# A two-layer transformer on one core: two weight splits and five modulation folds issued at other places

## The chip, the cores and the metric

The kernel runs on 1 core of a Trainium2 chip. The metric is the device time of one execution in microseconds. The engines are named as in the profile: PE is TensorE's matmul queue (PEld its weight loads), DVE VectorE, ACT ScalarE, POOL GpSimd, SP the queue that issues the DMAs. Each engine works through its own instructions in order and waits on semaphores for the others.

## The reference

Two layers over 512 latent tokens (`x`) and 256 context tokens (`ctx`), width 1024. Layer 0 mixes with attention, layer 1 with a gated recurrence (HGRN); each is followed by a SwiGLU feed-forward with a hidden width of 2816. Around both stand six modulation vectors, computed from the conditioning.

```python
for i in range(DEPTH):
    last = i == DEPTH - 1
    mod_l = (jax.nn.silu(c) @ ada_w[i] + ada_b[i])[:, None, :]
    mod_c = (jax.nn.silu(c_ctx) @ ada_w[i] + ada_b[i])[None, None, :]
    sh1_l, sc1_l, gt1_l, sh2_l, sc2_l, gt2_l = jnp.split(mod_l, 6, axis=-1)
    ...
    h = h + gt1_l * y_l
    h = h + gt2_l * swiglu(modulate(rms_norm(h, norm_ffn_w[i]), sh2_l, sc2_l), ffn_w_in[i], ffn_w_out[i])
    if not last:
        hc = hc + gt1_c * y_c
        hc = hc + gt2_c * swiglu(modulate(rms_norm(hc, norm_ffn_w[i]), sh2_c, sc2_c),
                                 ffn_w_in[i], ffn_w_out[i])
return rms_norm(h, final_norm_w)

def swiglu(h, w_in, w_out):
    a, u = jnp.split(h @ w_in, 2, axis=-1)
    return (jax.nn.silu(a) * u) @ w_out
```

## The kernel before, in words

**Products.** Every product is made of three matmuls (`mm3`, lines 118 to 120): each operand is split into a high part (a cast to fp32r on ACT, line 90) and a low part (the difference of the original and the high part, on DVE, line 95). `split` does this. With `late="h"` or `"l"` in its argument it pins the cast or the difference: a pinned instruction keeps its place in program order on its engine, while the scheduler may place the others by its own reckoning.

**The first feed-forward** (`ffn` for layer 0) treats the 768 tokens as two halves of 384 columns (`H`), and the 1024 inputs as two halves of four blocks (`b11`, `b12`, `b21`, `b22`: input half, token half). Hidden rows come in tiles `j` of 128. For `j` 0 and 1 the products are plain (`ffi`). From `j` = 2 on a hidden tile is a "pair" of gate and up weights, and is computed with seven block products in place of eight, by sums and differences: x, z, y, x again, w, y again, x again (`m1`, `m2`, `m5`, `m6`, `m4`, `m3`, `m7`). The operands of these are the four input blocks and four differences of them over the tokens, `t1` to `t4`; the differences are formed in place in `start_attention`, `b11 - b12` and `b22 - b12` on POOL (lines 1367 and 1371), then `-b11 - b22` and `-b22 - b21` on DVE (lines 1374 and 1378).

**Units.** The weights of a pair pass in seven units of 512 columns. A unit's `split_next()` makes its two parts in a ring of three tiles, then runs the unit's `after`: behind the first unit (`a11`) POOL makes three weight sums (lines 1220, 1220, 1223; the second of them is the weight of unit three, `raw_('w', 2, 1)`), behind the second (`a12`) a fourth (line 1228). All of these write over the tiles that the units read, so they come after the first two units' low parts. In `start_attention` the first two units are split after all token differences; `split_ahead(0)` splits some more behind the plain products. While `begun[0]` holds (in these start functions), the units' low parts are pinned and the casts are not.

**Around it.** When pair 2 begins, ACT and DVE also finish the hidden rows of tiles 0 and 1 (`plain_hidden`: SiLU at line 1057, the product `c` at line 1058, then `gh` and `gl`, the high and low part of the hidden rows), and split `t2`, `t4` and, before that, `t1`, `t3` (the tiles `xt1h`, `xt1l` and so on).

**Fill.** Between the units runs the fill: `ada_ffn` computes five chunks (0, 1, 2, 3 and 5) of layer 1's modulation on DVE, one step after another at given units. A chunk's steps end with a reduction to `adpart` (line 250). It is then "folded": four small matmuls sum its rows (`folded`, line 257; the profile counts two passes, so 8), and DVE adds the bias into `modc` (line 258). The fold of a chunk is issued some steps into the next chunk, and the last one after some empty steps or at the `drain()` at the end of the feed-forward.

The output products of a part of the hidden rows (`ffo`) follow the part's pairs; a row of them is 512 latent and 256 context columns, and DVE adds it to the residual `hT` (line 760).

## Time and profile before

| | |
|---|---|
| median of the runs | 1803.81 us (1802.84 to 1805.98, 3 runs) |
| profiled execution, span | 1806.6 us |
| PE busy | 1748.6 us, 97% |
| DVE, ACT, POOL busy | 1302.5, 871.2, 640.4 us |
| first feed-forward's pairs begin (first `x` product's end) | 475.1 us |
| third fold (line 257) | 773.7 us |
| the feed-forward's end (first `h` product of the next stage) | 965.5 us |

The profile is one execution, whose span lies 2.8 us above the median of the runs. In a row of the timeline the first number is the start in us from the span's start, the second the duration, then the engine, the line, what is written and read, the shape and how many such instructions the row groups; in brackets stands how long the engine was idle before and what ended it. PEclk is the granted clock of TensorE, 1.00 at full speed.

### The profile page before, as it was taken

The numbers are of one execution on the slowest core, as the hardware profiler recorded it, in microseconds if no ns is written. First come the engines' busy times: TensorE is split into PE (matmuls) and PEld (weight loads), VectorE is DVE, ScalarE is ACT, GpSimd is POOL, SyncE is SP. The second block draws the span as 40 slices with busy tenths as digits, with TensorE's granted clock in tenths as the row PEclk, the third lists the DMA queues.
The fourth block names the chain that finished last, engine by engine and source line by source line (L and its number), as shares of the span: only waits on it lengthen the run. The fifth ranks groups of instructions, "written<-read, shape, count | busy, mean of one in ns | idle before, by whom it ended". The sixth has DMA issues, their size and how long they took to land.

```text
span 1806.6 us, 30621 instructions
## 1 busy us (share of the span) xinstructions
PE 1748.6 (97%) x11717; PEld 1605.0 (89%) x11717; DVE 1302.5 (72%) x2269; ACT 871.2 (48%) x1777; POOL 640.4 (35%) x582
## 2 busy tenths in 40 slices
PE   8989999999999999999999999999999899999998
PEld 6788788898899989999998999899898899999996
DVE  4776688888888878887866555655747658786764
ACT  3454777777533424243346443333434445554444
POOL 1354355435512314121313333234425454333420
PEclk9999999999999999999999999999999899999999
DMA  8543410002034242545331122122211123333322
GB/s 297 202 129 116 153 36 25 24 1 77 24 111 122 71 129 88 159 129 158 96 114 46 59 71 68 51 83 83 80 49 47 57 59 114 100 111 103 100 61 83
DMA packets 213459, 166.43 MB, mean 92 GB/s; under 512 B 7953, under 2 KB 190401, under 8 KB 213313
## 3 DMA queue, kind: packets, MB, share of 16 engines
q1 hardware_dynamic: 213024, 163.43, 29.5%
q8 instruction: 92, 1.51, 0.3%
q10 hardware_dynamic: 288, 1.05, 0.1%
q14 instruction: 55, 0.44, 0.1%
HBM read 162.36 MB, written 2.10 MB: 91 GB/s over the span
## 4 chain that ended last, share of the span: by engine, by line
PE 78%; DVE 9%; ACT 4%; POOL 3%; issue 3%; DMA 2%; SPq 0%; POOLq 0%; DVEq 0%; ACTq 0%
PE ffo L120 5%; PE ffo L118 5%; PE ffo L119 5%; PE x L118 4%; PE x L120 4%; PE x L119 4%; PE pt L787 3%; PE y L120 2%; PE y L118 2%; PE y L119 2%; PE lv L1716 2%; PE hz L118 2%; PE hz L119 2%; PE hz L120 2%; PE sc L729 1%
## 5 line engine op out<-in xcount | busy, mean ns | idle before, releaser
L1723 POOL TENSOR_TENSOR KD<-KD,tot 128x384 f32<-128x384 f32 x96 | 102.7, 1092 | 81.8 <-ACT kc L1706 78.1
L777 POOL TENSOR_SCALAR pf<-pf,st 128x768 f32<-128x768 f32 (+1 forms) x96 | 73.3, 766 | 126.0 <-DVE st L776 89.5
L760 DVE SCALAR_TENSOR_TENSOR hT<-ffo,modc,hT 128x512 f32<-128x512 f32 (+1 forms) x122 | 78.6, 649 | 45.6 <-PE ffo L120 45.5
L120 PE MATMUL ffo<-gh,wlo_w 128*128 128x512 f32 (+1 forms) x304 | 103.2, 340 | 0.0
L119 PE MATMUL ffo<-gl,whi_w 128*128 128x512 f32 (+1 forms) x304 | 102.7, 338 | 0.0
L118 PE MATMUL ffo<-gh,whi_w 128*128 128x512 f32 (+1 forms) x304 | 102.4, 340 | 0.0
L242 DVE SCALAR_TENSOR_TENSOR adacc<-adw,csil,adacc 128x512 f32<-128x512 f32 x98 | 84.5, 871 | 7.9 <-DMA adw<-in_ada_w_dram 7.8
L95 DVE TENSOR_TENSOR ptl<-pt,pth 128x384 fp32r<-128x384 f32 (+1 forms) x160 | 79.9, 524 | 12.8 <-ACT pth L90 11.6
L90 ACT CAST pth<-pt 128x384 fp32r<-128x384 f32 (+1 forms) x160 | 69.7, 460 | 34.2 <-PE pt L787 22.5
L775 ACT ACTIVATE pf<-sc,st 128x768 f32<-128x768 f32 (+1 forms) x96 | 73.3, 764 | 19.0 <-DVE st L773 18.0
L1723 DVE TENSOR_TENSOR QD<-QD,tot 128x256 f32<-128x256 f32 x96 | 51.9, 581 | 41.2 <-PE lv L1716 41.2
L773 DVE TENSOR_REDUCE st<-sc 128x1 f32<-128x768 f32 (+1 forms) x96 | 74.2, 773 | 10.1 <-PE sc L730 8.7
L1706 ACT COPY kc<-KD 128x256 f32<-128x256 f32 x112 | 43.3, 413 | 75.9 <-PE lv L1716 45.8
L787 PE MATMUL pt<-ident,pf 128*128 128x128 f32 x448 | 72.1, 275 | 5.2 <-DVE ptl L95 4.1
L118 PE MATMUL ffo<-gh,foh 128*128 128x512 f32 (+1 forms) x186 | 71.4, 384 | 0.0
L120 PE MATMUL ffo<-gh,fol 128*128 128x512 f32 (+1 forms) x186 | 70.8, 381 | 0.2 <-DVE fol L95 0.2
L119 PE MATMUL ffo<-gl,foh 128*128 128x512 f32 (+1 forms) x186 | 70.9, 381 | 0.0
L1782 POOL TENSOR_SCALAR oss<-oss 128x4 f32<-128x4 f32 (+1 forms) x9 | 4.7, 522 | 181.8 <-DVE oss L1781 181.7
L1716 PE MATMUL lv<-QD,kc 128*128 128x128 f32 x448 | 63.4, 286 | 4.5 <-DVE QD L1723 2.4
L1716 PEld LDWEIGHTS lv<-QD,kc 128*128 128x128 f32 x448 | 58.6, 191 | 8.8 <-issue 4.6
L119 PEld LDWEIGHTS ffo<-gl,whi_w 128*128 128x128 f32 x304 | 57.8, 190 | 6.9
L787 PEld LDWEIGHTS pt<-ident,pf 128*128 128x128 f32 x448 | 51.2, 140 | 13.9 <-issue 6.4
(1114 smaller groups left out, 6794.1 us busy)
## 6 DMA issues: line engine op xcount, KB each, us to landing
adw<-in_ada_w_dram SPq DMA_DIRECT2D x40, 512.0 KB, 4.6
adw<-in_ada_w_dram SPq DMA_DIRECT2D x80, 256.0 KB, 2.8
raw_hz<-in_hgrn_w_in_dram SPq DMA_DIRECT2D x14, 512.0 KB, 3.7
adr<-in_ada_w_dram SPq DMA_DIRECT2D x16, 256.0 KB, 5.2
adr<-in_ada_w_dram SPq DMA_DIRECT2D x8, 512.0 KB, 7.7
raw_wq<-in_attn_w_qkv_dram SPq DMA_DIRECT2D x8, 512.0 KB, 6.8
raw_wo<-in_attn_w_o_dram SPq DMA_DIRECT2D x8, 512.0 KB, 3.5
raw_hv<-in_hgrn_w_in_dram SPq DMA_DIRECT2D x8, 512.0 KB, 4.9
```

What stands on the lines that cost most here:

```text
L95: m = (eng or DVE).tensor_tensor(lo, src, hi.bitcast(F32), op=ALU.subtract)
L118: PE.matmul(ps, ahi, bhi, start=first, stop=False, **kw)
L119: PE.matmul(ps, ahi, blo, start=False, stop=False, **kw)
L120: PE.matmul(ps, alo, bhi, start=False, stop=last, **kw)
L242: pin(DVE.scalar_tensor_tensor(a, raw, cc, a, op0=ALU.mult, op1=ALU.add))
L760: DVE.scalar_tensor_tensor(hT[o][:, a:e], ps, mcol(layer, ch, o, v), hT[o][:, a:e], op0=ALU.mult, op1=ALU.add)
L773: DVE.tensor_reduce(st3[:, 0:1], ps[:, :nk], op=ALU.max, axis=AX.X, negate=True)
L775: ACT.activation(pf, ps[:, :nk], AF.Exp, bias=st3[:, 0:1], accum_out=st3[:, 1:2])
L777: POOL.tensor_scalar(pf, pf, st3[:, 2:3], 1.0, op0=ALU.mult, op1=ALU.mult)
L787: PE.transpose(pt[:, i * P : (i + 1) * P], pf[:, (i0 + i) * P : (i0 + i + 1) * P], ident)
L1716: PE.matmul(ps[:, cs], kc[:, cs], mv, start=True, stop=True)
L1723: eng.tensor_tensor(view, view, f, op=ALU.mult)
```

## The change

Nothing is added and nothing taken out; three things stand elsewhere.

1. In `start_attention` two `split_next()` calls (units `a11` and `a12` of pair 2) stand ahead of the DVE differences `b22` and `b21`, where they stood behind them.
2. In layer 0, from the third unit on, the units split in the start function have their casts pinned as well as their low parts.
3. In `ada_ffn` a fold is issued 12 steps into the next chunk, where it was 5, and the last one waits for up to 12 empty steps.

```diff
@@ def split_next (line 1297)
-            split(g[0], g[1], u["src"](), late="l" if begun[0] else "")
+            split(g[0], g[1], u["src"](), late=("l" if layer or nsplit[0] < 2 else "hl") if begun[0] else "")
@@ def start_attention (from line 1369)
             for i in range(4):
                 b11, b12, b21, b22 = blocks(i)
                 pin(POOL.tensor_tensor(b12, b22, b12, op=ALU.subtract))
+            split_next()
+            split_next()
             for i in range(4):
                 b11, b12, b21, b22 = blocks(i)
                 pin(DVE.scalar_tensor_tensor(b22, b11, -1.0, b22, op0=ALU.mult, op1=ALU.subtract))
...
             for i in range(4):
                 b11, b12, b21, b22 = blocks(i)
                 pin(DVE.scalar_tensor_tensor(b21, b22, -1.0, b21, op0=ALU.mult, op1=ALU.subtract))
-            split_next()
-            split_next()
             xops["t3"] = operand("t3")
@@ def ada_ffn (from line 1523)
                 n += 1
-                if n == 5 and folded:
+                if n == 12 and folded:
                     folded()
                     folded = None
                 yield got
-        for _ in range(5):
+        for _ in range(12):
             yield
         folded()
```

What this moves in the engines' orders is shown at three places. The first is DVE ahead of pair 2: `x_5542` to `x_5581` are the four `b22` blocks, `c` the first half of hidden tile 0, and the row of `wlo_w` the low parts of the first two units.

```order
+L95 TENSOR_TENSOR wlo_w<-raw_('w', 2, 0)_5632,whi_w 128x512 x2
+L1376 SCALAR_TENSOR_TENSOR x_5542<-x_5461,x_5542 128x384
+L1376 SCALAR_TENSOR_TENSOR x_5553<-x_5478,x_5553 128x384
+L1376 SCALAR_TENSOR_TENSOR x_5570<-x_5495,x_5570 128x384
+L1376 SCALAR_TENSOR_TENSOR x_5581<-x_5531,x_5581 128x384
+L1058 TENSOR_TENSOR c_5796<-ffi,c_5796 128x384
 L95 TENSOR_TENSOR xt3l<-x_5461,xt3h 128x384
 L95 TENSOR_TENSOR xt3l<-x_5478,xt3h 128x384
```

Before, the order began with the four differences (then line 1374) and `c`, and the low parts stood here:

```order
-L1378 SCALAR_TENSOR_TENSOR x_5542<-x_5542 128x384
-L1378 SCALAR_TENSOR_TENSOR x_5553<-x_5553 128x384
-L1378 SCALAR_TENSOR_TENSOR x_5570<-x_5570 128x384
-L1378 SCALAR_TENSOR_TENSOR x_5581<-x_5581 128x384
-L95 TENSOR_TENSOR wlo_w<-raw_('w', 2, 0)_5632,whi_w 128x512 x2
```

The two low parts move 12 rows up, to right behind the last `xt1l`; all that stood between moves two instructions down. The order on POOL is the same, but its sums wait for these low parts.

The second place is ACT at the same time: `gh_5815` are the high parts of hidden tile 1, whose two halves come from `c_5842` and `c_5886`; `sw` and `raw_('w', 2, 1)` are weights that POOL has summed.

```order
 L1057 ACTIVATE c_5842<-ffi 128x384
 L1057 ACTIVATE c_5886<-ffi 128x384
-L90 CAST whi_w<-raw_('w', 2, 1)_5634 128x512
-L90 CAST whi_w<-sw_5798 128x512
 L90 CAST gh_5815<-c_5842 128x384
 L90 CAST whi_w<-raw_('w', 2, 1)_5634 128x512
+L90 CAST whi_w<-sw_5785 128x512
+L90 CAST whi_w<-raw_('w', 2, 1)_5634 128x512
 L90 CAST whi_w<-raw_('w', 2, 0)_5632 128x512
+L90 CAST gh_5815<-c_5886 128x384
 L1082 COPY c_5916<-x 128x384
-L90 CAST gh_5815<-c_5886 128x384
```

The cast of `gh` from `c_5842` now comes ahead of the casts of units three and four, behind which it stood, and the second `gh` ahead of the copy of the first product of pair 2.

The third place is PE at the third fold. Before, it stood between the 512 and the 256 columns of one row of output products:

```order
L120 MATMUL ffo<-gh_8254,wlo_w 128x512
L118 MATMUL ffo<-gh_8398,whi_w 128x512
L119 MATMUL ffo<-gl_8399,whi_w 128x512
L120 MATMUL ffo<-gh_8398,wlo_w 128x512
L257 MATMUL adc_8742<-adpart_8446,fold 32x8 x4
L118 MATMUL ffo<-gh_7970,whi_w 128x256
L119 MATMUL ffo<-gl_7971,whi_w 128x256
```

Now it stands within the pairs of the next part:

```order
L120 MATMUL y<-xb22h,wlo_w 128x384
L118 MATMUL y<-xb22h,whi_w 128x384
L119 MATMUL y<-xb22l,whi_w 128x384
L120 MATMUL y<-xb22h,wlo_w 128x384
L257 MATMUL adc_9180<-adpart_8446,fold 32x8 x4
L118 MATMUL x<-xt3h,whi_w 128x384
L119 MATMUL x<-xt3l,whi_w 128x384
```

The other four folds move by the same seven steps; the fifth now stands at the end of the feed-forward, right ahead of the first `h` product. The sixth (chunk 4, in the recurrence) stands where it stood.

## The prediction

> **What bounds the kernel now.** I read the page first, then TensorE's waits between 440 and 970 us, where every edit lies, then the timeline around the two longest of them. The page's busy shares and the engines of its chain of waits:

> ```profile
> PE 1748.6 (97%) x11717; PEld 1605.0 (89%) x11717; DVE 1302.5 (72%) x2269; ACT 871.2 (48%) x1777; POOL 640.4 (35%) x582
> ...
> PE 78%; DVE 9%; ACT 4%; POOL 3%; issue 3%; DMA 2%; SPq 0%; POOLq 0%; DVEq 0%; ACTq 0%
> ```

> TensorE is busy 1748.6 of 1806.6 us, so a reordering can only win from the 58 us in which it stands, and from matmuls that run at a lowered clock. Its waits in that stretch (the kind, us in total, times, longest):

> ```profile
> PE y L120 <- DVE wlo_w L95: 2.3, 1, 2.3
> PE adc L257 <- DVE adpart L250: 2.2, 1, 2.2
> ...
> PE h L118 <- DVE hT L760: 0.8, 1, 0.8
> PE y L118 <- ACT whi_w L90: 0.5, 1, 0.5
> PE w L119 <- DVE xt4l L95: 0.2, 1, 0.2
> ```

> Two places matter: **stall A**, the first product of pair 2 (y, at 478 us), and **stall B**, the third modulation fold (adc, at 774 us). Each is followed by matmuls at half clock, as stretches of 3.41 us show (after each engine its busy us; then PEclk):

> ```profile
> 476.46:479.88 3.42, 1.50 (x8) 0.86 (x6) 0.40 (x1) 2.08 (x5) 3.18 (x3) 1.00 0.00 0
> 479.88:483.29 3.41, 2.50 (x8) 2.50 (x9) 3.14 (x6) 1.22 (x4) 0.00 (x0) 0.50 0.03 9
> 483.29:486.70 3.41, 3.41 (x11) 2.88 (x10) 3.11 (x7) 3.14 (x8) 0.00 (x0) 0.50 0.49 145
> ...
> 770.07:773.48 3.41, 1.45 (x7) 0.83 (x5) 3.41 (x6) 0.00 (x0) 0.00 (x0) 1.00 0.59 173
> 773.48:776.90 3.42, 3.17 (x21) 3.17 (x22) 2.99 (x7) 0.18 (x1) 0.00 (x0) 0.50 0.45 111
> ```

> TensorE was busy 1.50 and 1.45 us of a stretch, and the next one or two ran at 0.50.

> **The folds, stall B.** TensorE and VectorE there:

> ```profile
> 771.13 0.39 PE L120 MATMUL ffo<-gh,wlo_w 128*128 128x512 f32 x1
> 771.66 0.70 DVE L249 STREAM_TRANSPOSE adt<-adacc 128x512 f32<-128x512 f32 x1
> 772.29 0.71 DVE L760 SCALAR_TENSOR_TENSOR hT<-ffo,modc,hT 128x512 f32<-128x512 f32 x1
> 772.91 0.67 DVE L250 TENSOR_REDUCE adpart<-adt 128x16 f32<-128x512 f32 x1
> ...
> 773.74 0.30 PE L257 MATMUL adc<-adpart,fold 128*32 128x8 f32 x8 [2.21 <-DVE adpart L250]
> 773.96 0.58 PE L118 MATMUL ffo<-gh,whi_w 128*128 128x256 f32 x1
> ...
> 776.69 0.42 PE L118 MATMUL x<-xb11h,whi_w 128*128 128x384 f32 x1
> ```

> The fold's eight small matmuls read a sum that VectorE finishes at 773.58 (772.91 + 0.67), while TensorE was free for them at 771.5. From 773.96 to 776.69 come the 12 matmuls of 256 columns of the last row, 0.23 apart; unthrottled they start 0.117 apart, 1.40 us for 12, as two steps in the same view show:

> ```profile
> 767.98 0.28 PE L119 MATMUL ffo<-gl,whi_w 128*128 128x256 f32 x1
> ...
> 768.21 0.29 PE L118 MATMUL ffo<-gh,whi_w 128*128 128x256 f32 x1
> ```

> So the wait costs 2.21 and the clock 2.73 - 1.40 = 1.33, together 3.5. In the changed order this fold stands seven fill steps later, after a y product, some 250 rows on, and reads a sum finished long before: no wait. Its own matmuls (0.22) go with it. What could give the 3.5 back is VectorE, which trails TensorE by some 2 us here (hT of the 771.13 group is written at 772.29): the next product starts at about 773.0 (776.69 less 3.5 and the fold's 0.22) instead of 776.69 and asks for its operands earlier. The product x needs none of VectorE's queue, and VectorE's row L258 of 0.16 leaves that queue too. I take -3.5. Bounds: -2.2 where the clock is not cut, 0 where the wait returns at the next product.

> The other four folds show no wait now and find their sums older than before: nothing. The fifth now drains at the end of the feed-forward, into a gap that is there already:

> ```profile
> 965.54 0.47 PE L118 MATMUL h<-hnb11h,whi_h 128*128 128x512 f32 x1 [0.82 <-DVE hT L760]
> ```

> Its 0.22 fits in that 0.82; if the cover is gone it costs 0.22, and its sum on VectorE 0.16. I take 0.

> **The split moved ahead, stall A.** What makes TensorE wait, in order: VectorE, GpSimd and ScalarE, then TensorE.

> ```profile
> 465.15 3.60 DVE L1374 SCALAR_TENSOR_TENSOR x<-x,x 128x384 f32<-128x384 f32 x4
> 468.67 0.55 DVE L1058 TENSOR_TENSOR c<-ffi,c 128x384 f32<-128x384 f32 x1
> 469.13 1.01 DVE L95 TENSOR_TENSOR xt3l<-x,xt3h 128x384 fp32r<-128x384 f32 x2
> ...
> 470.54 1.96 DVE L1378 SCALAR_TENSOR_TENSOR x<-x 128x384 f32<-128x384 f32 x4
> 472.41 1.28 DVE L95 TENSOR_TENSOR wlo_w<-raw_('w', 2, 0)_5632,whi_w 128x512 fp32r<-128x512 f32 x2
> ...
> 474.55 0.55 DVE L1058 TENSOR_TENSOR c<-ffi,c 128x384 f32<-128x384 f32 x1
> 479.48 0.66 DVE L95 TENSOR_TENSOR gl<-c,gh 128x384 fp32r<-128x384 f32 x1 [4.37 <-ACT gh L90]
> 480.06 0.68 DVE L95 TENSOR_TENSOR wlo_w<-raw_('w', 2, 1)_5634,whi_w 128x512 fp32r<-128x512 f32 x1
> ...
> 492.84 1.56 DVE L95 TENSOR_TENSOR wlo_w<-raw_('w', 3, 1)_5638,whi_w 128x512 fp32r<-128x512 f32 x1
> ```

> ```profile
> 462.17 5.22 POOL L1371 TENSOR_TENSOR x<-x,x 128x384 f32<-128x384 f32 x4
> 473.17 2.61 POOL L1220 TENSOR_TENSOR raw_('w', 2, 0)_5632<-raw_('w', 2, 0)_5632,raw_('w', 2, 1)_5634 128x512 f32<-128x512 f32 x1 [5.78 <-DVE wlo_w L95]
> 475.86 1.29 POOL L1220 TENSOR_TENSOR raw_('w', 2, 1)_5634<-raw_('w', 2, 1)_5634 128x512 f32<-128x512 f32 x1
> ...
> 492.11 1.74 POOL L1223 TENSOR_TENSOR sw<-raw_('w', 3, 0)_5636,raw_('w', 3, 1)_5638 128x512 f32<-128x512 f32 x1
> ```

> ```profile
> 477.19 0.62 ACT L90 CAST whi_w<-raw_('w', 2, 1)_5634 128x512 fp32r<-128x512 f32 x1 [5.83 <-POOL raw_('w', 2, 1)_5634 L1220]
> ```

> ```profile
> 475.10 0.33 PE L118 MATMUL z<-xb21h,whi_w 128*128 128x384 f32 x1
> ...
> 477.00 0.34 PE L120 MATMUL z<-xb21h,wlo_w 128*128 128x384 f32 x1
> ...
> 480.80 0.69 PE L120 MATMUL y<-xt1h,wlo_w 128*128 128x384 f32 x1 [2.32 <-DVE wlo_w L95]
> ...
> 488.22 0.45 PE L119 MATMUL w<-xt4l,whi_w 128*128 128x384 f32 x1 [0.24 <-DVE xt4l L95]
> ```

> At full clock matmuls start 0.173 apart (1.90 for 11). Without a stall, 12 of y and 12 of x after 477.17 bring w L119 to 481.50; it starts at 488.22. All of stall A is worth **6.7 us**.

> GpSimd's weight sums are the head of that chain: released by VectorE's low parts at 473.1, the second is done at 477.15, and ScalarE casts it. After the change those low parts stand 12 VectorE instructions earlier, so the sums can follow L1371 at about 467.5, 5.7 us sooner. [...] GpSimd's L1371 took 1.30 each (5.22 / 4) beside VectorE, which then needed 1.30 instead of 0.47 (the pace of L1378, 470.54 to 472.41 for four). A sum of 512 columns beside a low part of some 0.60 (two in 1.28) took 1.74, so it keeps VectorE out for about 1.74 - 0.60 = 1.14; the low part then took 1.56.

> [...]

> Before, three of the four sums ran in the 4.37 us in which VectorE waited; now all four meet its busiest stretch. With turns taken one by one: both low parts end at 468.0 (the second behind the last L1371, at 467.39); four rounds of 1.14 + 0.47 = 1.61 put the end of the last b22 difference at 474.45 and the first half's c at 474.9. From there, as before from 469.2 to 475.1 without the 1.2 of the low parts, 4.7: the second c ends at 479.6. Now the pin tells: ScalarE's gh of that c stands ahead of the cast of ('w', 2, 1). So gh ends at 480.1 and the cast at 480.6, though its input was ready at 470.8; VectorE's gl and low part follow, and y L120 starts at 481.4, 0.6 later than 480.80. After it the second gh now precedes the copy of x's bank, 0.4 more ahead of xt2h. So A goes from a stall behind GpSimd to one behind VectorE, at **+0.8** (bounds +0.6 and +1.0 by these steps, -6.7 if VectorE loses nothing). What is late next is y L118, by 3.4 us instead of 0.5.

> **Sum.** -3.5 + 0.8 = -2.7 on the profiled 1806.6, which lies 2.8 above the median of the runs; on the median, 1803.8 - 2.7 = **1801.1 us**.

> **Rivals.**
> 1. *The early sums do clear stall A.* For it: at 473.17 GpSimd asked while VectorE streamed and got in only after three more of its instructions (2.61 instead of 1.29), which cost VectorE nothing. Against: there GpSimd had been idle, now it comes straight out of L1371, as at 462 to 467, when they alternated. If half of the 4.6 us falls on VectorE, the second c ends at 477.4, y L120 starts near 479.2, 1.6 earlier, and the half clock shortens by one stretch (1.7): -3.3 - 3.5 gives 1797.0; if none does, 1803.8 - 6.7 - 3.5 = 1793.6. Chance 0.30.
> 2. *The fold gives less.* The wait returns at the next product (A +0.8, B 0: 1804.6), or the stretch in which the clock is judged lies so that the 2.21 is never punished (B -2.2: 1802.4). For the first, VectorE's lag; against, x needs nothing of it. Taken as 1803, chance 0.14.
> 3. *Slower.* z takes the bank that the first half's c frees, and my forecast frees it at 474.9, z's start being 475.10. If each sum keeps VectorE for its longest span, 1.74, and not 1.14, c ends at 477.3: z waits 2.2, y L120 starts 3.0 later than before, and one more stretch at half clock costs 1.7. With 0.4 for xt2h that is +5.1 - 3.5 = +1.6, 1805.4. It decides from an A of +3.5 on, and is told from no change only above +7.1, which needs the fold's gain to fail too. Chance 0.10.

> [...]

> **How the numbers follow.** Forecast 0.46, rivals 0.30, 0.14, 0.10. A change below 0.2% (3.6 us, here 1800.2) can't be told from none. Faster: most of rival 1 (0.27) and the third of the forecast where A costs less than reckoned (0.14), 0.41. Slower: 0.06, rival 3 where the fold fails too or its price is above what these rows give. Same: 0.53. The range runs from 1796.4, within rival 1, to 1804.6, the fold returning nothing; outside lie the full success and rival 3.

> **What would show it.** Right: no wait at L257, clock 1.00 at 773 to 777; GpSimd's L1220 at 467.5 and about 1.6 per sum; the b22 differences at 1.6 each; y L118 waiting about 3.4 for ScalarE's whi behind gh, y L120 near 481.4. Wrong: the b22 differences at 0.47 beside the sums, or y without a wait (rival 1); a wait at x, z or m3's sums near 773 to 786 (rival 2); a wait at z at 475 (rival 3).

## The result, and the profile after

| | before | after |
|---|---|---|
| median of 9 runs each | 1805.98 us (1802.84 to 1808.09) | 1802.55 us (1800.85 to 1804.49) |
| ratio | | 0.9982, 95% interval 0.9973 to 0.9990 |
| profiled execution, span | 1806.6 us | 1801.6 us |

In these runs the change was 3.4 us faster (1.8 to 4.9), where 2.7 was forecast. Measured a second time, beside other kernels (11 runs against 35 of before), the ratio was 0.9992 (0.9983 to 1.0001): -1.4 us, with no change at all still inside the interval. By either it lies within 0.2%, the bound that the prediction set for telling it from no change. The spans can't be set against each other as they stand: the time of an execution lies 1.8 us above its span (1803.39 to 1801.6 here), so the profiled execution of before would be one of 1808.4 by this estimate, slower than each of its nine runs.

The page's busy shares and chain are those of before but for small numbers:

```profile
PE 1747.4 (97%) x11717; PEld 1603.7 (89%) x11717; DVE 1306.6 (73%) x2269; ACT 870.9 (48%) x1777; POOL 641.0 (36%) x582
...
PE 77%; DVE 9%; ACT 4%; POOL 4%; issue 3%; DMA 2%; SPq 0%; POOLq 0%; DVEq 0%; ACTq 0%
```

TensorE's waits between 440 and 970 us tell more:

```profile
PE y L118 <- ACT whi_w L90: 3.2, 1, 3.2
PE rstd L304 <- DVE dg L300: 1.2, 1, 1.2
PE x L118 <- ACT c L1082: 0.9, 1, 0.9
PE h L118 <- DVE hT L760: 0.6, 1, 0.6
PE y L118 <- ACT c L1097: 0.6, 1, 0.6
PE w L119 <- DVE xt4l L95: 0.3, 1, 0.3
```

The wait at the fold (L257) is gone. The wait at pair 2 is not: it has moved from y L120, behind VectorE, to y L118, behind ScalarE's cast, and is longer (3.2 in place of 0.5 and 2.3). Two new ones have come, for ScalarE's copies at L1097 and L1082.

The whole of this execution runs about 5 us ahead of the profile of before, from its first 30 us on, long before anything that was changed; that is taken off when the two are compared. VectorE, GpSimd, ScalarE and TensorE at pair 2:

```profile
460.11 2.93 DVE L95 TENSOR_TENSOR wlo_w<-raw_('w', 2, 0)_5632,whi_w 128x512 fp32r<-128x512 f32 x2
462.96 6.32 DVE L1376 SCALAR_TENSOR_TENSOR x<-x,x 128x384 f32<-128x384 f32 x4
469.20 0.55 DVE L1058 TENSOR_TENSOR c<-ffi,c 128x384 f32<-128x384 f32 x1
...
473.88 0.55 DVE L1058 TENSOR_TENSOR c<-ffi,c 128x384 f32<-128x384 f32 x1
```

```profile
457.13 5.35 POOL L1371 TENSOR_TENSOR x<-x,x 128x384 f32<-128x384 f32 x4
462.45 1.73 POOL L1220 TENSOR_TENSOR raw_('w', 2, 0)_5632<-raw_('w', 2, 0)_5632,raw_('w', 2, 1)_5634 128x512 f32<-128x512 f32 x1
464.26 1.48 POOL L1220 TENSOR_TENSOR raw_('w', 2, 1)_5634<-raw_('w', 2, 1)_5634 128x512 f32<-128x512 f32 x1
465.70 1.60 POOL L1223 TENSOR_TENSOR sw<-raw_('w', 2, 0)_5632,raw_('w', 2, 1)_5634 128x512 f32<-128x512 f32 x1
467.38 1.48 POOL L1228 TENSOR_TENSOR raw_('w', 2, 0)_5632<-raw_('w', 2, 0)_5632,sw 128x512 f32<-128x512 f32 x1
```

```profile
474.46 0.51 ACT L90 CAST gh<-c 128x384 fp32r<-128x384 f32 x1 [2.57 <-DVE c L1058]
474.88 0.61 ACT L90 CAST whi_w<-raw_('w', 2, 1)_5634 128x512 fp32r<-128x512 f32 x1
```

```profile
475.54 0.69 PE L118 MATMUL y<-xt1h,whi_w 128*128 128x384 f32 x1 [3.24 <-ACT whi_w L90]
...
476.35 0.61 PE L120 MATMUL y<-xt1h,wlo_w 128*128 128x384 f32 x1
...
484.01 0.44 PE L119 MATMUL w<-xt4l,whi_w 128*128 128x384 f32 x1 [0.27 <-DVE xt4l L95]
```

The sums start right behind L1371 and take 1.48 to 1.73 each, and the four b22 differences need 6.32, 1.58 each where about 0.49 is their pace alone (no_sums, below): one engine's turn, then the other's. The input of the cast of ('w', 2, 1) is ready at 465.7 (464.26 + 1.48); the cast runs at 474.88, behind gh, for which ScalarE stood idle 2.57 us until VectorE had written c.

To see where time goes, each matmul's start in one execution was taken against the same matmul of before, in TensorE's order, the folds left out. "Start" is this difference at 130 us of before, "A" how it changes from 472 to 495 us, "B" from 760 to 778, "given back" from 778 to 900 (less than zero is earlier; worked out from the traces). The last column is the time that VectorE waited for adw transfers between 725 and 815 us, from its waits.

| execution | start | A | B | given back | adw waits |
|---|---|---|---|---|---|
| the change | -5.0 | +0.8 | -4.0 | +2.4 | 5.6 |
| after_again | -5.1 | +0.8 | -4.0 | +1.5 | 4.7 |
| split_only | -2.7 | +0.8 | +0.6 | +0.1 | 3.5 |
| folds_only | -5.3 | +0.3 | -4.0 | +2.3 | 5.5 |
| t3_late | -5.1 | +0.1 | -4.0 | 0.0 | 3.1 |
| third_early | -0.5 | +0.9 | -4.0 | +0.2 | 3.2 |
| no_sums | -1.7 | -3.5 | -4.0 | +1.6 | 4.8 |
| gl_late | -4.1 | -1.8 | -4.0 | +1.7 | 4.8 |
| gl_late_again | -4.1 | -0.3 | -4.0 | +1.6 | 4.7 |
| adw2 | -5.4 | +0.8 | -4.0 | +4.9 | 7.0 |
| adw4 | -3.0 | +0.8 | -4.0 | 0.0 | 1.4 |
| gl_adw4 | -3.4 | -0.3 | -4.0 | 0.0 | 1.2 |
| before_adw4 | -2.4 | 0.0 | +0.1 | 0.0 | 2.8 |

### The profile page after: what moved, and what is told of

The parts are those of the page before. It is cut to its first block, busy times and chain, and to the rows that moved or that the text cites. A ratio compares the mean times of both kernels' runs of the same rounds, so it can differ in the third digit from the quotient of the medians.

```text
span 1801.6 us, 30622 instructions
## 1 busy us (share of the span) xinstructions
PE 1747.4 (97%) x11717; PEld 1603.7 (89%) x11717; DVE 1306.6 (73%) x2269; ACT 870.9 (48%) x1777; POOL 641.0 (36%) x582
## 4 chain that ended last, share of the span: by engine, by line
PE 77%; DVE 9%; ACT 4%; POOL 4%; issue 3%; DMA 2%; SPq 0%; POOLq 0%; DVEq 0%; ACTq 0%
PE ffo L120 5%; PE ffo L118 5%; PE ffo L119 5%; PE x L118 3%; PE x L120 3%; PE x L119 3%; PE pt L787 3%; PE lv L1716 3%; PE y L120 2%; PE y L118 2%; PE y L119 2%; PE hz L118 2%; PE hz L119 2%; PE hz L120 2%; PE sc L729 1%
## 5 line engine op out<-in xcount | busy, mean ns | idle before, releaser
L760 DVE SCALAR_TENSOR_TENSOR hT<-ffo,modc,hT 128x512 f32<-128x512 f32 (+1 forms) x122 | 78.6, 649 | 45.1 <-PE ffo L120 45.1
L120 PE MATMUL ffo<-gh,wlo_w 128*128 128x512 f32 (+1 forms) x304 | 102.7, 338 | 0.0
L119 PE MATMUL ffo<-gl,whi_w 128*128 128x512 f32 (+1 forms) x304 | 102.3, 336 | 0.0
L118 PE MATMUL ffo<-gh,whi_w 128*128 128x512 f32 (+1 forms) x304 | 101.8, 338 | 0.0
L242 DVE SCALAR_TENSOR_TENSOR adacc<-adw,csil,adacc 128x512 f32<-128x512 f32 x98 | 83.4, 861 | 8.9 <-DMA adw<-in_ada_w_dram 8.8
L95 DVE TENSOR_TENSOR ptl<-pt,pth 128x384 fp32r<-128x384 f32 (+1 forms) x160 | 79.9, 524 | 12.8 <-ACT pth L90 11.6
L90 ACT CAST pth<-pt 128x384 fp32r<-128x384 f32 (+1 forms) x160 | 69.7, 460 | 34.2 <-PE pt L787 22.4
L118 PE MATMUL ffo<-gh,foh 128*128 128x512 f32 (+1 forms) x186 | 71.5, 384 | 0.0
L120 PE MATMUL ffo<-gh,fol 128*128 128x512 f32 (+1 forms) x186 | 70.9, 381 | 0.2 <-DVE fol L95 0.2
L119 PE MATMUL ffo<-gl,foh 128*128 128x512 f32 (+1 forms) x186 | 70.9, 381 | 0.0
L119 PEld LDWEIGHTS ffo<-gl,whi_w 128*128 128x128 f32 x304 | 57.3, 188 | 6.8
```

Of the source, the lines that this page charges most:

```text
L95: m = (eng or DVE).tensor_tensor(lo, src, hi.bitcast(F32), op=ALU.subtract)
L118: PE.matmul(ps, ahi, bhi, start=first, stop=False, **kw)
L119: PE.matmul(ps, ahi, blo, start=False, stop=False, **kw)
L120: PE.matmul(ps, alo, bhi, start=False, stop=last, **kw)
L242: pin(DVE.scalar_tensor_tensor(a, raw, cc, a, op0=ALU.mult, op1=ALU.add))
L760: DVE.scalar_tensor_tensor(hT[o][:, a:e], ps, mcol(layer, ch, o, v), hT[o][:, a:e], op0=ALU.mult, op1=ALU.add)
```

## The experiments

The theory: A costs 0.8 since GpSimd's sums and VectorE take turns; the folds give 4 at the fold, of which VectorE's lag takes some back. Two rivals: the split's move carries the gain, or the folds' gain stays whole.

### One part at a time

split_only has the moved splits and the pins, with the folds at 5 steps:

```diff
-                if n == 12 and folded:
+                if n == 5 and folded:
...
-        for _ in range(12):
+        for _ in range(5):
```

> The split move and the pin alone, folds as before. Theory (GpSimd and VectorE take turns, the stall only changes its releaser): y L118 waits 3.2 us for ScalarE's whi, w L119 starts 0.8 us later against the z product than before; the fold at L257 waits 2.2 us as before; time +0.8 us, within 1 us of before. Rival (the move wins, and what the two traces show is one execution's luck with the clock): 2 to 3 us faster than before.

Measured: ratio 0.9996 (0.9985 to 1.0007) to before. TensorE's waits, the two at issue:

```profile
PE y L118 <- ACT whi_w L90: 3.2, 1, 3.2
PE adc L257 <- DVE adpart L250: 2.7, 1, 2.7
```

A is +0.8 in its trace, the time is that of before. The interval runs from -2.7 to +1.3 us: it holds the theory's +0.8 and, at its edge, the smaller part of the rival's 2 to 3, so that the trace tells more than the runs.

folds_only is the kernel before with only `n == 12` and `range(12)`.

> The later folds alone, splits as before. Theory: no wait at L257, TensorE 4 us earlier at the x product behind it, 2.5 us of that given back within 25 us at two waits for ScalarE's copies (which stand behind VectorE's c); stall A as before with 2.3 us at y L120; time -1.5 us. Rival (the fold's wait carries the gain): -3.5 us, no new waits behind 774 us. Rival (the split carries it): 0 to -1 us.

Measured: 0.9981 (0.9971 to 0.9991), -3.4 us, as much as the change itself. Its waits:

```profile
PE y L120 <- DVE wlo_w L95: 2.3, 1, 2.3
...
PE x L118 <- ACT c L1082: 0.9, 1, 0.9
PE y L118 <- ACT c L1097: 0.7, 1, 0.7
```

The two new waits come with the folds alone, so they belong to B. The trace gives -4.0 + 2.3 = -1.7, as the theory had it, the runs -3.4; the interval (-1.6 to -5.2) just holds both.

### What stall A hangs on

no_sums leaves out GpSimd's four sums of pair 2. If VectorE takes turns with them, the four b22 differences fall from 6.32 us to 1.9 to 2.5, y L118 waits under 0.3 us, and the time falls by 4 to 6:

```diff
             def sums():
                 sw.append(fp.tile([P, 512], F32, tag="sw", bufs=2, name=f"sw{j}"))
+                if begun[0] and not layer:
+                    POOL.memset(sw[0], 0.0)
+                    return
...
             def sum4():
+                if begun[0] and not layer:
+                    return
```

> The change without GpSimd's four weight sums of pair 2 (left out; a memset stands for the tile sw, so the first feed-forward's hidden tile 2 is not the reference's). [...] Rival (VectorE is late by its own work): the differences take 6 us as before and y L118 waits 3 us.

Measured: 0.9976 (0.9966 to 0.9987), 1799.73 us; after_again, in the same batch, 1802.56. VectorE:

```profile
466.16 1.95 DVE L1381 SCALAR_TENSOR_TENSOR x<-x,x 128x384 f32<-128x384 f32 x4
...
472.72 0.54 DVE L1058 TENSOR_TENSOR c<-ffi,c 128x384 f32<-128x384 f32 x1
```

The differences take 1.95 in place of 6.32, y starts without a wait, and A is -3.5, 4.4 below the change. So the sums that run beside the differences are what the split's move pays with. The medians differ by 2.8 and not by 4 to 6; with intervals of 1.8 us to each side this neither confirms nor contradicts the trace's 4.4.

t3_late takes work out of VectorE's queue ahead of y; third_early also splits unit three ahead of the b21 differences:

```diff
             xops["t3"] = operand("t3")
-            for i in range(4):
+            for i in range(2):
                 xsplit("t3", i, x[i][:, H:n])
...
+            if i == 2 and not layer:
+                for k in range(2, 4):
+                    xsplit("t3", k, x[k][:, H:n], late="hl")
             split_ahead(min(i + 1, len(units) - 1))
```

> The change, with the splits of the third and fourth block of t3 pinned behind those of t4 (0.94 us of VectorE and 0.83 us of ScalarE work out of the chain ahead of y). Theory (stall A is VectorE's queue up to the second c): y L118 starts about 0.9 us earlier and waits 2.3 instead of 3.2, w L119 0.9 earlier; time -0.9 us against the change. Rival (GpSimd's sums or ScalarE set it): y L118 waits 3.2 as before.

Measured: 0.9971 (0.9957 to 0.9986, 7 runs; the change did not run beside it, so the -0.9 can't be read from the times).

```profile
PE y L118 <- ACT whi_w L90: 2.3, 1, 2.3
```

The wait is 2.3 us instead of 3.2, as VectorE's queue says, and A is 0.7 below the change's. The edit takes work from ScalarE's queue as well, but ScalarE was the one that waited there (2.57 us for c, in the rows of the change).

```diff
             plain_hidden(0, 1, *ps0)
+            split_next()
             for i in range(4):
                 b11, b12, b21, b22 = blocks(i)
```

> t3_late, and unit three split ahead of the b21 differences, so that its cast and low part are ready before y. Theory (VectorE is the bound up to xt4l): y L118 and L120 start without a wait, but x L119 then waits 3 to 4 us for xt2l, and w L119 starts no more than 0.5 us earlier than in t3_late; the time is that of t3_late within 0.5 us plus what the half clock does. Rival (only the cast behind gh held TensorE): w L119 3 us earlier than in the change, time -3 us against it.

Measured: 0.9990 (0.9978 to 1.0002). y has no wait any more, but the next product has all of it, one matmul earlier than expected and for ScalarE's high part:

```profile
PE x L118 <- ACT xt2h L90: 4.6, 1, 4.6
```

ScalarE's order there, with what it waited for:

```profile
481.95 0.51 ACT L90 CAST gh<-c 128x384 fp32r<-128x384 f32 x1 [1.39 <-DVE c L1058]
482.37 0.47 ACT L1082 COPY c<-x 128x384 f32<-128x384 f32 x1
482.74 1.75 ACT L90 CAST xt2h<-x 128x384 fp32r<-128x384 f32 x4
```

A is +0.9, no better than the change. With the cast behind gh out of the way TensorE stands one product later for what VectorE's queue has not reached: the rival (the cast alone held it) falls.

gl_late is t3_late with the split of hidden tile 1 pinned behind that of t2:

```diff
+            if defer is not None:
+                defer.append((gh[j][:, h * H : h * H + H], gl[j][:, h * H : h * H + H], c))
+                return
             split(gh[j][:, h * H : h * H + H], gl[j][:, h * H : h * H + H], c)
...
+                if i == 0:
+                    for d in deferred:
+                        split(*d, late="hl")
```

> t3_late, and the split of hidden tile 1 (gh and gl, both halves) pinned behind t2's splits, so that neither ScalarE's casts of units three to six nor VectorE's low parts stand behind it. Theory (stall A is VectorE's queue, plus 0.58 us twice for the way over gh): y L118 about 0.4 us earlier than in t3_late, xt2l and xt4l 1.5 to 2.5 us earlier, w L119 1.5 to 2.5 us earlier against z than in t3_late; time -2 us against t3_late, -4 against the change. Rival (the clock or ScalarE sets it): w L119 as in t3_late.

Measured: 0.9980 (0.9971 to 0.9989), 1801.14 us, 1.4 below after_again and not 4. Run again:

> gl_late once more, on the chip of the two runs with four buffers. Theory: 0.998 of before, as in its first run; the given-back time behind 774 us goes with L242's waits.

Measured: 0.9977 (0.9968 to 0.9985), 1800.94 us. In both executions y L118 no longer waits; y L120 waits 1.5 us for its low part and w L118 1.6 for ScalarE's xt4h. With the same waits A is -1.8 in the one and -0.3 in the other. In the traces of before and of the change the granted clock changes only at whole multiples of 3.413 us from its other changes (in before from 19.11 to 1800.87 us, 522 of them apart, in the change from 474.78 to 1795.74, 387 apart). In the first execution of gl_late it goes back to full at 101.89 and to half at 1426.26, 388 of them apart, so the stretches between these borders can be laid out. The first execution and then the second:

```profile
477.35:480.77 3.42, 2.20 (x11) 1.88 (x11) 3.42 (x8) 2.19 (x5) 0.00 (x0) 1.00 0.55 150
480.77:484.18 3.41, 2.39 (x12) 2.14 (x13) 3.41 (x8) 3.41 (x9) 2.39 (x1) 1.00 0.52 151
```

```profile
479.76:483.18 3.42, 1.56 (x8) 1.11 (x7) 3.42 (x8) 3.03 (x8) 1.37 (x1) 1.00 0.19 56
483.18:486.59 3.41, 3.41 (x13) 3.41 (x12) 3.41 (x5) 1.27 (x3) 3.33 (x2) 0.50 0.34 102
```

The same stall falls across two stretches in the first, which leaves TensorE busy for 2.20 and 2.39 us of them, and mostly into one in the second, which leaves 1.56. Half clock follows only there, for one stretch (0.50 from 483.18 to 486.59), and the two A lie 1.5 us apart: against t3_late's +0.1, w L119 is 1.9 earlier in the one, as expected, and 0.4 in the other. The two kernels are the same, so where the borders lie against the work is not the order's doing.

### What gives the folds' gain back

> The change itself once more, beside the three runs below on one chip. Theory: 0.998 of before (the folds' -3.4 us, nothing from the split); in its trace y L118 waits 3.2 us, and how much is given back behind 774 us goes with the time that VectorE's L242 waits for the adw transfers between 725 and 815 us: 2 us and more where these are over 5 us, none where they are near 3 us. Rival (the giving back belongs to the changed order): it comes whatever L242 waits.

Measured: 0.9992 (0.9983 to 1.0001), A +0.8, B -4.0, given back 1.5 at adw waits of 4.7. The rows of the first execution of the change show the way: VectorE, then ScalarE, then TensorE.

```profile
752.41 0.75 DVE L242 SCALAR_TENSOR_TENSOR adacc<-adw,csil,adacc 128x512 f32<-128x512 f32 x1 [2.68 <-DMA adw<-in_ada_w_dram]
...
774.01 0.75 DVE L242 SCALAR_TENSOR_TENSOR adacc<-adw,csil,adacc 128x512 f32<-128x512 f32 x1 [0.91 <-DMA adw<-in_ada_w_dram]
...
776.03 0.75 DVE L242 SCALAR_TENSOR_TENSOR adacc<-adw,csil,adacc 128x512 f32<-128x512 f32 x1 [0.87 <-DMA adw<-in_ada_w_dram]
...
778.56 0.55 DVE L1088 TENSOR_TENSOR c<-z,c 128x384 f32<-128x384 f32 x1
```

```profile
779.15 0.49 ACT L1089 ACTIVATE z<-c 128x384 f32<-128x384 f32 x1 [5.30 <-DVE c L1088]
779.58 0.47 ACT L1097 ACTIVATE c<-y 128x384 f32<-128x384 f32 x1
```

```profile
780.10 0.44 PE L118 MATMUL y<-xb22h,whi_w 128*128 128x384 f32 x1 [0.64 <-ACT c L1097]
```

The fill's L242 waited for its transfer at the head of VectorE's queue (2.68, 0.91 and 0.87 us in these rows); behind it stood c (L1088), for which ScalarE's SiLU stood idle 5.30 us, and behind that ScalarE's copy of y, for which TensorE's next y waited 0.64. adw2 and adw4 change the number of buffers for the transfers, and with it the places that the scheduler finds for the fill. In adw4 two of VectorE's fill rows between 725 and 815 us stand one place earlier, and the orders of TensorE, ScalarE and GpSimd are the change's. In adw2 VectorE's fill rows from 742 to 780 us stand 1 to 7 places later, and some of ScalarE's near 790 have changed places, so that it changes more than the waits. The edit of adw4:

```diff
-                raw = fp.tile([P, 512], F32, tag="adraw", bufs=3, name=f"adw{layer}{ch}{hf}{k}")
+                raw = fp.tile([P, 512], F32, tag="adraw", bufs=4, name=f"adw{layer}{ch}{hf}{k}")
...
-            accs = [acc_n[:, 0:512] if wide else
+            accs = [acc_n[:, 0:512] if wide or v else
...
-            ahead = 2 if wide else 3
+            ahead = 2 if wide else 4
```

(adw2 has 2 in both places and leaves `accs` alone.)

> The change with two buffers for the adw tiles in place of three, each transfer asked for one tile later. Theory (what the folds gain is given back where VectorE waits for adw): L242's waits over the first feed-forward double at least (from 8.8 us), TensorE's waits behind 774 us for ScalarE's copies grow from 1.5 to 3 us and more, time 1 to 6 us longer than the change. Rival (VectorE's lag comes from its own work): no longer than the change within 1 us.

Measured: 1.0011 (0.9999 to 1.0022), 2.5 us above after_again. L242 waited 14.0 us in all, against 7.9 in after_again: more, but not double. VectorE's wait between 725 and 815 us, TensorE's behind 774, and the stretch that came next:

```profile
DVE adacc L242 <- DMA adw<-in_ada_w_dram: 7.0, 11, 2.2
```

```profile
PE y L118 <- ACT c L1097: 2.1, 1, 2.1
```

```profile
793.00:796.40 3.40, 1.28 (x8) 0.96 (x6) 2.41 (x5) 1.71 (x5) 0.00 (x0) 1.00 0.33 113
796.40:799.80 3.40, 3.40 (x11) 3.40 (x12) 2.60 (x4) 1.36 (x3) 2.06 (x2) 0.51 0.53 152
```

One wait of 2.1, not the 3 expected, but the stretch around it is followed by half clock: 4.9 us are given back, more than the folds brought. The changed order has a part in this that no run separates.

> The change with four buffers for the adw tiles in place of three (the second accumulator lies in acc_n, which is free there). Theory: L242's waits between 725 and 815 us fall from 4.7 to under 3 us, the two waits for ScalarE's copies behind 774 us are gone, the 4 us that TensorE gains at the third fold stay; time 1 to 2.5 us below the change. Rival (the lag is VectorE's own work): the same waits, the same time.

Measured: 0.9980 (0.9971 to 0.9989), 1801.40 us, 1.2 below after_again's median of another batch; the intervals overlap. The trace is clearer. Nothing is given back, no wait for ScalarE's copies is left behind 774 us, and VectorE waits 1.4 us in all:

```profile
DVE adacc L240 <- DMA adw<-in_ada_w_dram: 1.2, 1, 1.2
...
DVE adacc L242 <- DMA adw<-in_ada_w_dram: 0.2, 1, 0.2
```

Taken with the table, what is given back follows the adw waits through the eleven executions with the later folds, in both the orders of pair 2 and with 2, 3 and 4 buffers: 0.0 to 0.2 up to 3.2 us, 1.5 to 1.7 at 4.7 and 4.8, 2.3 and 2.4 at 5.5 and 5.6, 4.9 at 7.0 (adw2, with its changed order and half clock). adw4 and gl_adw4, where little but the waits changed, show that it is a cause and not only a companion. The rival, that it belongs to the order, falls: t3_late and third_early have the change's order there and gave back 0.0 and 0.2.

> The kernel before with the four adw buffers. Theory (the fold waits since VectorE runs 2 us behind, of which adw's waits are a part): the wait at L257 falls from 2.2 to about 1 us and may escape the clock's cut; -1 to -2.5 us against before. Rival (the fold simply comes too soon behind its sum): L257 waits 2.2 us still, time as before.

Measured: 0.9984 (0.9975 to 0.9993); L257 still waits 2.1 us in its trace, and neither A nor B moves against before. The fold came too soon behind its sum, buffers or not. What made the runs 2.9 us faster its trace doesn't show, and can't well show: the profiled execution was the slowest of the twelve, 1806.95 us where their median is 1802.39. That stays open.

> gl_late with the four adw buffers. Theory: both gains add, -4 us against the change (1798.5 where that is 1802.5). Rival: they overlap, no faster than gl_late.

Measured: 0.9977 (0.9969 to 0.9986), 1800.85 us and not 1798.5; gl_late_again beside it 1800.94. In the traces B is whole in the one (0.0 given back) and not in the other (1.6), but the runs don't tell them apart. t3_late, gl_late, gl_adw4 and adw4 are the fastest versions with the full computation, 0.9971 to 0.9980 of before; their intervals overlap those of the change, so that none of them is shown to beat it.

## Why the prediction came out as it did

**Stall A was right, step by step.** With the 5.04 us of this execution's head start added, c of the first half ended at 474.8 (forecast 474.9), the second c at 479.5 (479.6), gh at 480.0 (480.1), y L118 started after 3.2 (3.4), y L120 at 481.4 (481.4), and A is +0.8 (+0.8) in all five executions with exactly that order of pair 2 (the change, after_again, split_only, adw2, adw4). The price of a sum's turn, 1.14 from one row, gave rounds of 1.61; they took 1.58. no_sums shows the cause, third_early that VectorE's queue and not the cast is the bound.

**The folds: right mechanism, one step wrong.** The wait at L257 and the cut clock are gone (1.00 from 481.61 to 1386.14 us in the change), and B is -4.0 in every execution with the later folds, 0.5 more than reckoned: beside the wait (2.21) and 12 matmuls at half clock (1.33), the fold's own matmuls and the first of x, at half clock too, left the path there. The step that failed is the one that let the gain stand: "The product x needs none of VectorE's queue". True of x; but y, the sixth product from there, needs ScalarE's copy behind VectorE's c, and the x product with t2 of the next pair another. There 1.5 to 2.4 came back in six of the eleven executions with the later folds; of the change's 2.4, 0.9 came in at that y and 1.2 at that x. Rival 2 had the return of a wait, at a chance of 0.14, though at the next product and all or nothing; its signs even named m3, which is this y. It is a part, and it goes with the transfers. In the traces the change nets +0.8 - 4.0 + 1.5 to 2.4, so -0.8 to -1.7; the two measurements of -3.4 and -1.4 lie around the forecast of -2.7, and the later is nearer to the traces. That the sum came so close is in part luck: it left out a loss of 1.5 to 2.4, and what the first measurement shows beyond the traces' -1.7 is not explained.

**The others.** Rival 1, the early sums clearing stall A, did not come: GpSimd came straight out of L1371 and turns were taken, as the prediction argued against it. Rival 3 did not come either; z was ready 0.3 us ahead of need (c ended at 469.75, z started at 470.06). The half clock after stall A stayed, as taken, but how long it lasted did not matter to A: it was two stretches in the change (0.50 from 474.78 to 481.61 us) and one in after_again (0.51 from 476.46 to 479.88), A is +0.8 in both, and both have the same 0.3 us wait of w for VectorE's xt4l. The fifth fold at the end cost nothing: h's wait fell from 0.8 to 0.6 with the fold inside it.

**What the numbers hid.** The ground under the sum is wide: the starts in the table scatter from -5.4 to 0 between executions, from the first 130 us, which no kernel here touched. Against that a term of 0.8 can be checked in a trace, not in the times.

## What to carry to other kernels

Moving GpSimd's work earlier did not help here, since VectorE had no gap there (460.11 to 474.43 us in the change): the time that both needed added up (1.58 us a difference beside a sum, 0.49 without), and the wait came back under another engine's name. A stall that is removed shortens the time in which the trailing engine catches up: follow its queue for several products, and look there for instructions that wait for a transfer, since VectorE's waits for adw were passed on here (5.6 us of them with 2.4 given back in the change, 1.4 with none in adw4). For changes of a few us, line up two traces instruction by instruction; the medians of some ten runs did not tell terms of one or two us apart.

## What the runs showed of the hardware beyond that

With the stretches laid out between the clock's own changes, as for gl_late above, half clock followed one with TensorE busy for 0.93 us in the change:

```profile
471.37:474.78 3.41, 0.93 (x6) 0.61 (x4) 3.06 (x7) 0.84 (x3) 0.00 (x0) 1.00 0.00 0
474.78:478.20 3.42, 2.66 (x8) 2.43 (x9) 3.20 (x6) 2.27 (x5) 0.00 (x0) 0.50 0.00 0
```

In the change GpSimd's sums of pair 2, which came straight behind other GpSimd instructions, and VectorE's differences took turns (1.58 us a round), while the first sum of pair 3, which came out of 14.71 us of idle time, ended only behind four of VectorE's low parts:

```profile
483.57 2.94 POOL L1220 TENSOR_TENSOR raw_('w', 3, 0)_5636<-raw_('w', 3, 0)_5636,raw_('w', 3, 1)_5638 128x512 f32<-128x512 f32 x1 [14.71 <-DVE wlo_w L95]
```

```profile
483.40 1.96 DVE L95 TENSOR_TENSOR xt4l<-x,xt4h 128x384 fp32r<-128x384 f32 x4
485.28 1.52 DVE L240 TENSOR_SCALAR adacc<-adw,csil 128x512 f32<-128x512 f32 x1
```

The sum took 2.94 us, where one took 1.29 in a gap of VectorE's (the second L1220 row of before). The four low parts kept their pace of 0.47 beside it; L240 behind them took 1.52, where it took 0.48 at 770.12.

The start differed by up to 5.4 us between executions of kernels that are the same there. In two profiles TensorE waits for the first transfers for different times, before and then the change, within the first 130 us:

```profile
PE pa L187 <- DMA adr<-in_ada_w_dram: 4.4, 3, 3.0
```

```profile
PE pa L187 <- DMA adr<-in_ada_w_dram: 2.1, 4, 1.2
```

Of the 5.0 us between these two that is 2.3. Before also ran at half clock from 19.1 to 25.9 us, and the change did not; what that accounts for is open.
